# A streaming-encoder block on one core: operand offsets modulo 512 bytes, and four early steps of the output projection

## The chip, the cores and the metric

The kernel runs on one core of a Trainium2 chip. Its five engines have instruction streams of their own: TensorE (PE; its weight loads are listed apart as PEld), VectorE (DVE), ScalarE (ACT), GpSimd (POOL) and SyncE (SP), which here only issues transfers. The metric is the device time of one execution in microseconds, the median of the runs. All matmuls here have fp32 operands that were split into a high and a low fp32r part, so that each product is three matmuls: high·high, high·low, low·high.

## The reference

One Mamba-2 (SSD) mixer and one squared-ReLU MLP, each post-normalised, on a sequence of 1024 tokens with model width 1024:

```
h  = x * (1 + sc1) + sh1
zxbcdt = h @ w_in                      # 1024 -> 2048 (z) + 4096 (x, B, C) + 32 (dt)
xbc = silu(conv4(xbc)); dt = softplus(dt + bias)
y  = chunked SSD scan, 16 chunks of 64, 8 groups; y = y + d_skip * xs
y  = gated_rmsnorm(y, z) ; y = y @ w_out          # 2048 -> 1024
x  = layer_norm(ALPHA * x + g1 * y)
h  = x * (1 + sc2) + sh2
x  = layer_norm(ALPHA * x + g2 * (relu(h @ w1)**2 @ w2))   # 1024 -> 4096 -> 1024
```

The vectors sh, sc and g come from `silu(c) @ ada_w + ada_b`, which the kernel computes too, in blocks, beside the other work.

## The kernel before, in words

**Stages.** The head (to about 72 us) modulates x and computes dt. Then the input projection runs to about 725 us: 45 column tiles of `w_in` on line L146 (left operand `hi` or `lo`, right operand `hh` or `hl`, the split h), with the scan of group after group between its matmuls (L332 to L384) and a gate per half group (L392 to L420), which writes y to DRAM. The last gates, (7,0) and (7,1), run after the last projection; the gate's sum over channels is a pair of matmuls `pr` (L404, L405) on `sh` and `sl`.

**The output projection** follows, in four passes of `out_pass(T, Dh, po)`: T is the half of the tokens, Dh the half of the output columns. A pass has 16 steps k of 128 channels, each 12 matmuls of 128x512 on L559: four token tiles by three products, `lhsT` a piece of y, `rhs` the weights. Steps 14 and 15 come together at the end, since they need the last gates. `out_load` brings a step's weights (`owr`, 256 KB) and y (`yr`) in over SP; ScalarE casts the high part (L119), GpSimd subtracts for the low part of the weights (`owl`, L122), VectorE for that of y. y's split tiles are called `b11`, `b21` and so on after the blocks in which they lie: the same memory later holds h2, the MLP's input. In pass (0,0) the first two steps don't use `out_load`: their weights and y (both called early, `yx`) are loaded before the projection ends, into buffers of the projection's own pool.

Pass (0,1) does the other columns for the same tokens. It loads y's steps 0 and 1 again, now as `b` tiles. Beside it run two blocks of the modulation, `mods_ln1` (L594 to L607): 8 loads `adm`, a chain of 8 VectorE instructions (L600, L602), and then four one-column matmuls on L606 whose right operand is a column of ones. The tiles of `adm` share 8 buffers, so the second block's loads wait until the first block's chain and matmuls have read them. Passes (1,0) and (1,1) take the other tokens, with y in plain tiles `y0_k`, `y1_k` for k below 8 and in `b` tiles above.

**The MLP.** The first two weight tiles of `w1` are loaded and split into `w1h`, `w1l` by `forms1` (GpSimd subtracts, L122) while pass (1,1) runs. L713 then multiplies plainly, with some weights in tiles `ph`, `pl`; L804 has the larger part of the up-projection, in products of sums of blocks (7 products in place of 8, operands `t..`, `s..`, `b..`, `w1..`, 1176 matmuls); L918 has the down-projection, from about 1270 us.

**What sets the order.** Instructions are written in the order of the code, with a list `work` that is popped between projection tiles; the scheduler then orders each engine's stream by its own estimate, and a tile's buffer (pool, tag, `bufs`) makes its next user wait for its last reader. `issue_after(x)` keeps an instruction behind x.

**Where operands lie.** [...] The place of an operand in it modulo 512 bytes, of the left one against the right one, is as follows in the program built: L146 480/480, L918 both equal (480, 96 or 256), L559 with `b` tiles equal, L713 with `ph`, `pl` equal. Unequal are L804 (224 bytes apart, all 1176 matmuls), L713 with `w1h`, `w1l` (224 apart, 96 matmuls), L559 with the plain `y` tiles of passes (1,0) and (1,1) (224 apart, 192 matmuls), the early steps with `yx` (288 apart, 24 matmuls) and the head's L230 (288 apart, 160 matmuls). In most pairs of the first kind both operands lie in the same half of the partition's memory, in most of the second in different halves; L230's both lie in the upper half.

## Time and profile before

| | us |
|---|---|
| median of 3 runs (lowest, highest) | 1626.96 (1625.54, 1627.66) |
| the profiled execution | 1625.36 |
| its span | 1623.6 |
| TensorE busy | 1564.5 |
| VectorE, ScalarE, GpSimd busy | 984.7, 784.0, 561.4 |
| pass (0,0): first matmul to last | 725.6 to 787.9 |
| pass (0,1) | 787.9 to 839.6 |
| passes (1,0) and (1,1) | 839.6 to 931 |

The profile shows one execution, so durations are summed against its 1625.36 us, 1.6 us below the median. TensorE's matmuls are pipelined: the listed length of one (0.39 or 0.40 us) is longer than the distance from one start to the next, and it is the distance that counts in a row of them. Idle time of TensorE stands in the view of waits with what ended it. The granted clock is 1.00 at 2.4 GHz and 0.50 at 1.2 GHz.

### The profile page before, as it was taken

Reading aid. Unit: us, or ns where it says so; the run is one execution under the profiler, and the core shown is the slowest. Engines: PE = TensorE matmul, PEld = TensorE weight load, DVE = VectorE, ACT = ScalarE, POOL = GpSimd, SP = SyncE. Lnnn points to the kernel's source line nnn. Section 1 sums busy time; section 2 is a strip of 40 time slices with the busy share of each in tenths; the row PEclk is TensorE's granted clock in tenths of the full one; section 3 lists DMA queues with packets and bytes.
Section 4 is the critical chain, followed back from the end, with each engine's and each line's share of the span. In section 5 each row is a group of like instructions: output and inputs, shape, how many; then the busy total and the mean of one; then the engine's idle time right before and its main releaser. Section 6 shows DMA issues by size and latency. Waiting matters only on the chain.

```text
span 1623.6 us, 20290 instructions
## 1 busy us (share of the span) xinstructions
PE 1564.5 (96%) x7600; PEld 1263.0 (78%) x7600; DVE 984.7 (61%) x1473; ACT 784.0 (48%) x1183; POOL 561.4 (35%) x306
## 2 busy tenths in 40 slices
PE   6999999999999999998999999999999999999997
PEld 5887777878787888875787877888888888878886
DVE  8757886676768656747853356655554642296335
ACT  3546587575757676865334236333333323233230
POOL 3323424242333333244446607233332222244121
PEclk9999999999999999998999999999999999999999
DMA  8324422322323222215856413333334555436531
GB/s 323 138 76 135 143 98 79 104 88 83 116 66 121 67 88 64 79 33 169 287 165 210 130 65 104 118 115 105 104 117 159 205 183 175 151 139 224 172 124 52
DMA packets 78193, 209.89 MB, mean 129 GB/s; under 512 B 9744, under 2 KB 11280, under 8 KB 77200
## 3 DMA queue, kind: packets, MB, share of 16 engines
q1 hardware_dynamic: 76752, 204.91, 37.8%
q0 software_dynamic: 1056, 3.67, 0.6%
q8 instruction: 60, 0.98, 0.2%
q14 instruction: 37, 0.30, 0.1%
q10 hardware_dynamic: 288, 0.03, 0.0%
HBM read 175.41 MB, written 33.16 MB: 128 GB/s over the span
## 4 chain that ended last, share of the span: by engine, by line
PE 76%; DVE 10%; DMA 6%; ACT 4%; issue 2%; POOL 1%; SPq 0%; DVEq 0%; POOLq 0%; ACTq 0%
PE mm L146 22%; PE mm L918 20%; PE mm L804 17%; PE mm L559 6%; PE mm L713 3%; DMA adr<-in_ada_r_dram 2%; DVE mac L437 2%; PE py L364 2%; PE pst L377 1%; PE py L369 1%; PE mm L230 1%; DVE xs L159 1%; DMA yr<-y_dram 1%; DVE macc L205 1%; DMA ada<-in_ada_a_dram 1%
## 5 line engine op out<-in xcount | busy, mean ns | idle before, releaser
L146 PE MATMUL mm<-hh,whi 128*128 128x512 f32 x720 | 288.1, 400 | 0.0
L146 PE MATMUL mm<-hl,whi 128*128 128x512 f32 x720 | 286.4, 398 | 0.0
L146 PE MATMUL mm<-hh,wlo 128*128 128x512 f32 x720 | 286.1, 397 | 0.0
L918 PE MATMUL mm<-w2h,uh 128*128 128x512 f32 x512 | 197.9, 389 | 1.2 <-DVE tm L953 1.2
L918 PE MATMUL mm<-w2l,uh 128*128 128x512 f32 x512 | 198.2, 389 | 0.0
L918 PE MATMUL mm<-w2h,ul 128*128 128x512 f32 x512 | 197.1, 389 | 0.0
L122 POOL TENSOR_TENSOR wlo<-wraw,whi 128x1024 fp32r<-128x1024 f32 (+1 forms) x47 | 113.6, 2419 | 224.4 <-ACT whi L119 224.4
L146 PEld LDWEIGHTS mm<-hl,whi 128*128 128x128 f32 x720 | 136.4, 190 | 29.7 <-issue 2.2
L146 PEld LDWEIGHTS mm<-hh,whi 128*128 128x128 f32 x720 | 136.3, 189 | 29.3 <-issue 2.1
L146 PEld LDWEIGHTS mm<-hh,wlo 128*128 128x128 f32 x720 | 136.2, 189 | 28.8 <-issue 2.1
L358 POOL TENSOR_TENSOR ea<-ea,Ct 128x512 f32<-128x512 f32 x56 | 78.4, 1399 | 183.7 <-ACT ea L357 144.8
L122 POOL TENSOR_TENSOR w2l<-w2r,w2h 128x1024 fp32r<-128x1024 f32 x30 | 75.5, 2520 | 185.1 <-ACT w2h L119 185.1
L122 DVE TENSOR_TENSOR ul<-ur,uh 128x512 fp32r<-128x512 f32 x62 | 50.2, 818 | 125.8 <-ACT uh L119 125.6
L122 POOL TENSOR_TENSOR owl<-owr,owh 128x512 fp32r<-128x512 f32 x62 | 87.6, 1422 | 82.9 <-ACT owh L119 82.8
L918 PEld LDWEIGHTS mm<-w2h,uh 128*128 128x128 f32 x512 | 96.1, 188 | 21.7 <-DVE tm L953 1.6
L119 ACT CAST uh<-ur 128x512 fp32r<-128x512 f32 x62 | 38.3, 621 | 153.2 <-PE mm L918 124.3
L352 ACT ACTIVATE dec<-ar,acs 128x128 f32<-128x128 f32 x256 | 81.6, 390 | 62.5 <-PE py L364 59.2
L918 PEld LDWEIGHTS mm<-w2l,uh 128*128 128x128 f32 x512 | 96.1, 188 | 20.1
L918 PEld LDWEIGHTS mm<-w2h,ul 128*128 128x128 f32 x512 | 96.1, 188 | 19.7
L159 DVE SCALAR_TENSOR_TENSOR xs<-mm,convw,xs 128x1023 f32<-128x1023 f32 (+2 forms) x45 | 57.5, 1278 | 35.4 <-ACT xs L153 34.7
L119 ACT CAST owh<-owr 128x512 fp32r<-128x512 f32 x62 | 38.2, 619 | 78.3 <-PE mm L559 38.0
L119 ACT CAST w2h<-w2r 128x1024 fp32r<-128x1024 f32 x62 | 64.8, 1048 | 23.3 <-DMA w2r<-in_w_dram 18.2
(407 smaller groups left out, 3493.8 us busy)
## 6 DMA issues: line engine op xcount, KB each, us to landing
w2r<-in_w_dram SPq DMA_DIRECT2D x62, 512.0 KB, 3.8
wraw<-in_w_in_dram SPq DMA_DIRECT2D x45, 512.0 KB, 3.9
w1r<-in_w_dram SPq DMA_DIRECT2D x34, 512.0 KB, 3.7
ar<-a_dram SPq DMA_DIRECT2D x64, 256.0 KB, 3.2
owr<-in_w_out_dram SPq DMA_DIRECT2D x62, 256.0 KB, 3.1
ur<-u_dram SPq DMA_DIRECT2D x62, 256.0 KB, 2.8
u_dram<-row SPq DMA_DIRECT2D x28, 512.0 KB, 3.8
adr<-in_ada_r_dram SPq DMA_DIRECT2D x24, 512.0 KB, 3.5
```

Source lines behind the costliest of these rows:

```text
L119: return (act.copy if eng is act else eng.tensor_copy)(hi, src)
L122: return eng.tensor_tensor(lo, src, hi.bitcast(F32), op=ALU.subtract)
L146: pe.matmul(ps[:, hf, :], lhsT=w_[:, k, :], rhs=x_[:, k, ts], start=(k == 0 and i == 0), stop=(k == KT - 1 and i == 2))
L159: vec.scalar_tensor_tensor(dst[:, j:S], src[:, 0:S - j], convw[:, ct, 3 - j:4 - j], dst[:, j:S], op0=ALU.mult, op1=ALU.add)
L352: act.activation(dec[:, h, :], ar[:, h, :], AF.Relu, scale=-1.0, bias=acs[:, c, g * HPG + h:g * HPG + h + 1])
L358: pool.tensor_tensor(ea, ea, G["C"][:, ts].unsqueeze(1).broadcast_to([P, HPG, C]), op=ALU.mult)
L364: pe.matmul(py[i * HD:(i + 1) * HD, j, :], lhsT=X[:, h, :], rhs=dec[:, h, :], start=True, stop=(c == 0))
L437: vec.scalar_tensor_tensor(acc, ad[:, i, :], csil[:, k:k + 1], acc, op0=ALU.mult, op1=ALU.add)
L559: mm_ = pe.matmul(po[t // 2][:, t % 2, :], lhsT=l_[:, t * P:t * P + P], rhs=r_, start=(k == 0 and i == 0), stop=(k == 15 and i == 2))
L713: pe.matmul(ups[T, f // 2][:, f % 2, :], lhsT=w_[:, k, :], rhs=x_[:, k % 4, :], start=(k == 0 and i == 0), stop=(k == KT - 1 and i == 2))
L804: pe.matmul(dst, lhsT=w_[:, k, :], rhs=x_[:, k, :], start=(first and k == 0 and i == 0), stop=(k == 3 and i == 2), skip_group_check=not first)
L918: pe.matmul(po[t][:, Dh, :], lhsT=l_[:, t * P:(t + 1) * P], rhs=r_[:, Dh * 512:Dh * 512 + 512], start=(f == 0 and i == 0), stop=(f == NF - ...
```

## The change

1. **Offsets.** A function `offset(pool, n)` puts a tile of n bytes ahead in a pool (and clears it with one VectorE instruction): 288 bytes in the head's pool `hdp`, 224 in `mpa`. In the program built, L804, L713, L559 with `y` tiles and L230 then have their two operands at equal offsets modulo 512 bytes. The early steps' pairs stay 288 apart, and there are now 48 such matmuls.
2. **Four early steps.** Steps 0 to 3 of pass (0,0) are loaded and split ahead of the projection's end (tiles `wx`, `yx`); `wx` of step 0 and 1 share their buffers with the raw loads of steps 3 and 2, and `wx` of 2 and 3 take the tags of `whi` and `wlo`. Steps 4 to 7 of that pass are loaded into `spare` tiles, which have the memory of `b11`. `b11` is taken after the pass, so y's steps 0 to 3 (two more than before) are loaded and split again in pass (0,1).
3. **The table.** After the last projection's Silu, ScalarE loads the table that has both Ln and Exp.
4. **L606** (now L636) must come behind step 13 of its pass.
5. **`forms1`** lets VectorE make `w1l` of the first two tiles.

The listings below are one engine's instructions in program order: row number, line, operation, output and inputs. TensorE behind the projection, before: the end of the two steps on `yx` (24 matmuls from row 2861), then the pair `pr` of the next half gate, and step 2 on `b11`.

```order
2873 L559 MATMUL mm<-whi,yx 128x512
2874 L559 MATMUL mm<-wlo,yx 128x512
2875 L559 MATMUL mm<-whi,yx 128x512 x2
2876 L559 MATMUL mm<-wlo,yx 128x512
2877 L559 MATMUL mm<-whi,yx 128x512
2878 L404 MATMUL pr<-sh,ones_r 128x512
2879 L405 MATMUL pr<-sl,ones_r 128x512
2880 L559 MATMUL mm<-owh,b11h 128x512 x2
2881 L404 MATMUL pr<-sh,ones_r 128x512
2882 L559 MATMUL mm<-owl,b11h 128x512 x2
2883 L559 MATMUL mm<-owh,b11l 128x512
```

The same place now:

```order
2860 L410 MATMUL pr<-sl,ones_r 128x512
2861 L585 MATMUL mm<-wx,yx 128x512 x12
2862 L585 MATMUL mm<-wx,yx_6312 128x512 x6
2863 L585 MATMUL mm<-wx,yx_6313 128x512 x2
2864 L585 MATMUL mm<-wx,yx 128x512 x12
2865 L585 MATMUL mm<-wx,yx_6312 128x512 x6
2866 L585 MATMUL mm<-wx,yx_6313 128x512 x10
2867 L409 MATMUL pr<-sh,ones_r 128x512
2868 L585 MATMUL mm<-owh,b21h 128x512 x2
2869 L410 MATMUL pr<-sl,ones_r 128x512
2870 L585 MATMUL mm<-owl,b21h 128x512
```

Forty-eight matmuls in a row stand between the last gate pair of the projection and the next one, where 24 stood; the third `pr` pair, which stood two matmuls behind the second, stands at row 2899, 30 rows on.

TensorE in pass (0,1) before, where the first four one-column matmuls of the modulation stand (the second four are at row 3162):

```order
3110 L559 MATMUL mm_6797<-owh,b21h 128x512
3111 L559 MATMUL mm_6797<-owl,b21h 128x512
3112 L559 MATMUL mm_6797<-owh,b21l 128x512
3113 L606 MATMUL mm<-one_131,adm 128x1 x4
3114 L559 MATMUL mm_6796<-owh,b21h 128x512
3115 L559 MATMUL mm_6797<-owh,b21h 128x512
3116 L559 MATMUL mm_6796<-owl,b21h 128x512
```

The same four now, behind step 13 of the pass:

```order
3189 L585 MATMUL mm_6792<-owh,b22l 128x512
3190 L585 MATMUL mm_6791<-owh,b22h 128x512
3191 L585 MATMUL mm_6792<-owh,b22h 128x512
3192 L636 MATMUL mm<-one_131,adm 128x1 x4
3193 L585 MATMUL mm_6791<-owl,b22h 128x512
3194 L585 MATMUL mm_6791<-owh,b22l 128x512
```

They moved from the first third of the pass to its last steps. The second four now, where pass (1,0) begins on `y_0`:

```order
3213 L585 MATMUL mm_6792<-owl,b22h 128x512
3214 L585 MATMUL mm_6792<-owh,b22l 128x512
3215 L636 MATMUL mm<-one_131,adm 128x1 x4
3216 L585 MATMUL mm<-owh,y_0_7269 128x512
3217 L585 MATMUL mm<-owl,y_0_7269 128x512
```

They are the last instruction of pass (0,1), and the rows between the two fours hold 22 matmuls.

GpSimd in passes (1,0) and (1,1), before (`h_n` is a tile of h2, `owl` the low part of a step's weights):

```order
108 L122 TENSOR_TENSOR b21l<-h_7207,b21h 128x512
109 L122 TENSOR_TENSOR b21l<-h_7224,b21h 128x512
110 L122 TENSOR_TENSOR owl<-owr,owh 128x512 x3
111 L122 TENSOR_TENSOR w1l<-w1r,w1h 128x1024
112 L122 TENSOR_TENSOR owl<-owr,owh 128x512
113 L122 TENSOR_TENSOR w1l<-w1r,w1h 128x1024
114 L122 TENSOR_TENSOR b21l<-h_7241,b21h 128x512
115 L122 TENSOR_TENSOR b21l<-h_7258,b21h 128x512
116 L122 TENSOR_TENSOR owl<-owr,owh 128x512 x16
```

The same place of GpSimd now:

```order
108 L126 TENSOR_TENSOR b21l<-h_7210,b21h 128x512
109 L126 TENSOR_TENSOR b21l<-h_7227,b21h 128x512
110 L126 TENSOR_TENSOR owl<-owr,owh 128x512 x4
111 L126 TENSOR_TENSOR b21l<-h_7244,b21h 128x512
112 L126 TENSOR_TENSOR b21l<-h_7261,b21h 128x512
113 L126 TENSOR_TENSOR owl<-owr,owh 128x512 x16
```

It has nothing but `owl` and `b21l` left there. VectorE in the same passes now, where `forms1`'s two subtractions went:

```order
863 L126 TENSOR_TENSOR b11l<-h_7236,b11h 128x512
864 L123 CAST b11h<-h_7253 128x512
865 L126 TENSOR_TENSOR b11l<-h_7253,b11h 128x512
866 L126 TENSOR_TENSOR w1l<-w1r,w1h 128x1024
867 L577 TENSOR_TENSOR owr<-owr,g1b 128x512
868 L126 TENSOR_TENSOR w1l<-w1r,w1h 128x1024
869 L577 TENSOR_TENSOR owr<-owr,g1b 128x512 x2
870 L680 TENSOR_TENSOR tm<-mm,g1b 128x512 x2
```

They are its rows 866 and 868: VectorE makes `w1l` ahead of the multiplications `owr*g1b` of pass (1,1)'s weights.

The diff:

```diff
--- before.py
+++ after.py
@@ -47,6 +47,10 @@
 
     def const(shape, name, dt=F32):
         return con.tile(shape, dt, name=name, tag=name)
+
+    def offset(pl_, n):
+
+        vec.memset(pl_.tile([P, n // 4], F32, name="offset", tag="offset", bufs=1), 0.0)
 
     phA = ExitStack()
     ca = phA.enter_context(tc.tile_pool(name="ca", bufs=1, reuse_waits="tile"))
@@ -166,6 +170,7 @@
     hd = ExitStack()
     psh = hd.enter_context(tc.tile_pool(name="psh", bufs=1, space=PSUM))
     hdp = hd.enter_context(tc.tile_pool(name="hdp", bufs=2, reuse_waits="tile"))
+    offset(hdp, 288)
     hring = gp.tile([P, 2, S], F32, name="hring", tag="zt", bufs=1)
     hps = [psm.tile([P, 2, 512], F32, name="mm", tag="mm") for _ in range(2)]
     hps.append(psh.tile([P, 2, 512], F32, name="mmh", tag="mmh"))
@@ -453,7 +458,10 @@
         if j == 0:
             groups[g]["z"] = gp.tile([P, 2, S], F32, name="zt", tag="zt", bufs=1)
         ps = proj(2 * g + j)
-        act.activation(groups[g]["z"][:, j, :], ps.rearrange("p a b -> p (a b)"), AF.Silu)
+        sz = act.activation(groups[g]["z"][:, j, :], ps.rearrange("p a b -> p (a b)"), AF.Silu)
+        if (g, j) == (NG - 1, 1):
+            with tc.issue_after(sz.ins):
+                act.preload_act_table_set("natural_log_exp_and_others")
 
     work = []
 
@@ -488,16 +496,30 @@
         pop(int(debt))
         debt -= int(debt)
 
-    yx = gp.tile([P, 2, S], F32R, name="yx", tag="xs")
+    yx = [gp.tile([P, 2, S], F32R, name="yx", tag="xs"), gp.tile([P, S], F32R, name="yx2", tag="Bt"),
+          gp.tile([P, S], F32R, name="yx3", tag="Ct")]
+    raws = [None] * 4
+    wx = [None] * 4
+
+    def early_load(k):
+        raws[k] = wp.tile([P, 2, 512], F32, name="wraw", tag="wraw", bufs=4)
+        sp.dma_start(raws[k][:, 0, :], a["w_out"][k][:, 0:512])
+        sp.dma_start(raws[k][:, 1, :], y_dram[k][:, 0:512])
+
     early = []
-    for k in range(2):
-        raw = wp.tile([P, 2, 512], F32, name="wraw", tag="wraw", bufs=4)
-        sp.dma_start(raw[:, 0, :], a["w_out"][k][:, 0:512])
-        sp.dma_start(raw[:, 1, :], y_dram[k][:, 0:512])
-        w = [wp.tile([P, 512], F32R, name="w" + q, tag="w" + q) for q in ("hi", "lo")]
-        y = (yx[:, k, 0:512], yx[:, k, 512:S])
-        split(raw[:, 0, :], *w, act, pool)
-        split(raw[:, 1, :], *y, act, vec)
+    early_load(0)
+    early_load(1)
+    for k in range(4):
+        tg = "wraw" if k < 2 else "whi" if k == 2 else "wlo"
+        wx[k] = wp.tile([P, 2, 512], F32R, name="wx", tag=tg, **(dict(bufs=4) if k < 2 else {}))
+        if k == 1:
+            early_load(2)
+            early_load(3)
+    for k in range(4):
+        w = (wx[k][:, 0, :], wx[k][:, 1, :])
+        y = [(yx[0][:, k, :] if k < 2 else yx[k - 1])[:, i * 512:i * 512 + 512] for i in range(2)]
+        split(raws[k][:, 0, :], *w, act, pool)
+        split(raws[k][:, 1, :], *y, act, vec)
         early.append((w, y))
     phR.close()
 
@@ -510,7 +532,9 @@
 
         return [per.tile([P, 4, 512], F32R, name=nm + q, tag=nm + q) for q in "hl"]
 
-    B = {(kh, T): h2_block(f"b{kh + 1}{T + 1}") for T in range(2) for kh in range(2)}
+
+    spares = [per.tile([P, 4, 512], F32, name="spare" + q, tag="b11" + q) for q in "hl"]
+    B = {(kh, T): h2_block(f"b{kh + 1}{T + 1}") for T in range(2) for kh in range(2) if T + kh}
 
     def rstd_of(pl_, var, n, nm):
 
@@ -539,11 +563,13 @@
     def out_load(T, Dh, k):
 
         ds_ = slice(Dh * 512, Dh * 512 + 512)
-        wr = ob_pool.tile([P, 512], F32, name="owr", tag="owr", bufs=3)
+        spare = T == 0 and Dh == 0 and 4 <= k < 8
+        wr = (spares[0][:, k - 4, :] if spare else
+              ob_pool.tile([P, 512], F32, name="owr", tag="owr", bufs=3))
         queue["w"] = sp.dma_start(wr, a["w_out"][k][:, ds_]).ins
         yr = None
-        if (Dh == 0 and not (T == 0 and k >= 14)) or (T == 0 and k < 2):
-            yr = ob_pool.tile([P, 512], F32, name="yr", tag="yr")
+        if (Dh == 0 and not (T == 0 and k >= 14)) or (T == 0 and k < 4):
+            yr = spares[1][:, k - 4, :] if spare else ob_pool.tile([P, 512], F32, name="yr", tag="yr")
             sp.dma_start(yr, y_dram[k][:, T * 512:T * 512 + 512])
         wh = ob_pool.tile([P, 512], F32R, name="owh", tag="owh", bufs=3)
         wl = ob_pool.tile([P, 512], F32R, name="owl", tag="owl", bufs=3)
@@ -564,7 +590,7 @@
     def out_pass(T, Dh, po):
         ws = []
         for k in range(16):
-            first = T == 0 and Dh == 0 and k < 2
+            first = T == 0 and Dh == 0 and k < 4
             ws.append(early[k][0] if first else out_load(T, Dh, k))
             ks = [k] if k < 16 - KL else range(16 - KL, 16) if k == 15 else []
             for t in range(4):
@@ -573,10 +599,12 @@
             if Dh == 0 and T == 1 and k % 4 == 0:
                 load_row(4 + k // 4)
 
-    yt0 = yt = [y_tiles(0, k) for k in range(16)]
+    yt0 = yt = [None] * 4 + [y_tiles(0, k) for k in range(4, 16)]
     po = [psm.tile([P, 2, 512], F32, name="mm", tag="mm") for _ in range(2)]
     pop(len(work))
     out_pass(0, 0, po)
+    B[0, 0] = h2_block("b11")
+    yt[0:4] = [y_tiles(0, k) for k in range(4)]
     sbA.close()
     phA.close()
 
@@ -584,6 +612,7 @@
     lnp = ctx.enter_context(tc.tile_pool(name="lnp", bufs=1, reuse_waits="tile"))
     up_ = ExitStack()
     mpa = up_.enter_context(tc.tile_pool(name="mpa", bufs=2, reuse_waits="tile"))
+    offset(mpa, 224)
     rowp = up_.enter_context(tc.tile_pool(name="rowp", bufs=4, reuse_waits="tile"))
     hk = up_.enter_context(tc.tile_pool(name="hk", bufs=1, reuse_waits="tile"))
     q7t = lambda: hk.tile([P, 512], F32, name="q7", tag="q7")
@@ -602,8 +631,9 @@
                 vec.scalar_tensor_tensor(t_, t_, csil[:, k:k + 1], ad[-1], op0=ALU.mult, op1=ALU.add)
             ad.append(t_)
         pm = psm.tile([P, 2, 512], F32, name="mm", tag="mm")
-        for i in range(4):
-            pe.matmul(pm[:, 0, i:i + 1], lhsT=ad[-1][:, i * P:(i + 1) * P], rhs=one1, start=True, stop=True)
+        with tc.issue_after(queue["k13"]):
+            for i in range(4):
+                pe.matmul(pm[:, 0, i:i + 1], lhsT=ad[-1][:, i * P:(i + 1) * P], rhs=one1, start=True, stop=True)
         mod2_add(b, pm[:, 0, 0:4])
 
     rows = {}
@@ -685,7 +715,7 @@
     po = [psm.tile([P, 2, 512], F32, name="mm", tag="mm") for _ in range(2)]
     out_pass(1, 0, po)
     out_evict(1, 0, po, sts)
-    ws1 = [forms1(load1(f)) for f in range(2)]
+    ws1 = [forms1(load1(f), eng=vec) for f in range(2)]
     po = mm2()
     out_pass(1, 1, po)
     out_evict(1, 1, po, sts)
```

## Rows read from the trace of the kernel before

**Rows 1.** The page's first part: busy time, share of the span, instructions.

```profile
PE 1564.5 (96%) x7600; PEld 1263.0 (78%) x7600; DVE 984.7 (61%) x1473; ACT 784.0 (48%) x1183; POOL 561.4 (35%) x306
```

**Rows 2.** Windows of lines L804 and L918: length, PE busy (x), PEld busy (x), clock, DMA.

```profile
987.00:1270.00 283.00, 275.14 (x1176) 220.82 (x1176) 1.00 0.34 118
...
1290.00:1600.00 310.00, 308.80 (x1362) 255.35 (x1362) 1.00 0.48 161
```

**Rows 3.** Timeline of TensorE, lines L713 and L230: start us, us, instruction.

```profile
970.89 0.40 PE L713 MATMUL mm<-b12h,w1h 128*128 128x512 f32 x1
...
972.06 0.40 PE L713 MATMUL mm<-b12l,w1h 128*128 128x512 f32 x1
...
984.66 0.39 PE L713 MATMUL mm<-b12h,ph 128*128 128x512 f32 x1
...
986.02 0.39 PE L713 MATMUL mm<-b22h,ph 128*128 128x512 f32 x1
...
48.23 0.39 PE L230 MATMUL mm<-hh,wh 128*128 128x512 f32 x1
...
50.80 0.40 PE L230 MATMUL mmh<-hh,wl 128*128 128x512 f32 x1
```

**Rows 4.** Waits of TensorE from 700 to 1000 us: in total, times, longest.

```profile
PE mm L559 <- POOL owl L122: 3.7, 2, 3.1
PE mm L559 <- ACT b11h L119: 3.6, 1, 3.6
...
PE mm L606 <- DVE adm L602: 2.9, 1, 2.9
PE pr L404 <- DVE sh L119: 2.7, 2, 1.6
...
PE pr L405 <- DVE sl L122: 1.4, 1, 1.4
...
PE mm L559 <- POOL wlo L122: 0.6, 1, 0.6
```

**Rows 5.** Windows of line L559 in three stretches at half clock: columns as in Rows 2.

```profile
736.80:747.00 10.20, 5.33 (x11) 3.64 (x12) 0.50 0.29 91
...
808.50:811.90 3.40, 3.40 (x9) 2.66 (x8) 0.50 0.99 333
...
887.00:890.40 3.40, 2.95 (x7) 2.37 (x8) 0.50 0.37 93
```

**Rows 6.** Windows, all engines: PE, PEld, DVE, ACT, POOL busy, clock, DMA share, GB/s.

```profile
725.60:787.90 62.30, 53.70 (x248) 40.63 (x247) 42.22 (x58) 37.29 (x63) 31.42 (x25) 0.92 0.52 165
787.90:839.60 51.70, 47.80 (x209) 38.76 (x208) 34.00 (x42) 14.74 (x26) 22.82 (x16) 0.97 0.72 249
729.00:747.00 18.00, 9.52 (x25) 5.97 (x25) 13.26 (x18) 9.85 (x16) 7.41 (x8) 0.72 0.36 118
```

**Rows 7.** Timeline of ScalarE around the last projection: start, us, instruction, idle before.

```profile
724.88 1.03 ACT L456 ACTIVATE zt<-mm 128x1024 f32<-128x1024 f32 x1 [7.09 <-PE mm L146]
```

**Rows 8.** DMA issues between 780 and 850 us: KB each, median us to landing.

```profile
adm<-in_ada_r_dram SPq DMA_DIRECT2D x16, 256.0 KB, 5.2
```

**Rows 9.** Timeline of VectorE, the modulation chain, and its last rows before 890 us.

```profile
797.88 8.19 DVE L602 SCALAR_TENSOR_TENSOR adm<-adm,csil 128x512 f32<-128x512 f32 x7
...
886.30 1.64 DVE L551 TENSOR_TENSOR owr<-owr,g1b 128x512 f32<-128x512 f32 x1 [6.09 <-POOL b21l L122]
```

**Rows 10.** Timeline of GpSimd, 877 to 889 us.

```profile
877.26 2.40 POOL L122 TENSOR_TENSOR w1l<-w1r,w1h 128x1024 fp32r<-128x1024 f32 x1 [2.21 <-ACT w1h L119]
...
881.33 2.39 POOL L122 TENSOR_TENSOR w1l<-w1r,w1h 128x1024 fp32r<-128x1024 f32 x1
883.68 2.50 POOL L122 TENSOR_TENSOR b21l<-h,b21h 128x512 fp32r<-128x512 f32 x2
886.13 2.95 POOL L122 TENSOR_TENSOR owl<-owr,owh 128x512 fp32r<-128x512 f32 x2
```

**Rows 11.** Timeline of ScalarE, the cast that one of those subtractions waits for.

```profile
879.88 1.14 ACT L119 CAST b21h<-h 128x512 fp32r<-128x512 f32 x2
```

## The prediction

> **What bounds the kernel now.** I read the page's busy times first, and the reader is to see one number: TensorE works 1564.5 of 1623.6 us, 96% [rows 1]. So an edit pays only if TensorE's matmuls come closer together, if one of its idle gaps closes, or if a stretch at half clock goes. I then read three views for these three.
>
> For the distance I read windows of single lines. L804 is busy 275.14 us for 1176 matmuls, 234.0 ns each; L918, with the same shape and the same full clock, 308.80 us for 1362, 226.7 ns [rows 2]. TensorE doesn't wait in either, so something else parts them. The timeline has both values on one line: on L713 five distances with `w1h`, `w1l` take 972.06 − 970.89 = 1.17 us (234 ns), six with `ph`, `pl` 986.02 − 984.66 = 1.36 us (227 ns) [rows 3]. The left operands are of the same kind there; what differs is where the right one lies. L230 has eleven distances in 50.80 − 48.23 = 2.57 us, 234 ns, though both its operands lie in the same half [rows 3].
>
> For the gaps I read TensorE's waits from 700 to 1000 us. Those that the change touches are 8.3 us behind the projection (`b11h` 3.6, `sh` 2.7, `sl` 1.4, `wlo` 0.6), 2.9 for L606 on the `adm` chain, and one of 3.1 for `owl` [rows 4]. Around the first group 18.00 us hold only 9.52 of matmuls [rows 6]. With each of the three groups goes a stretch at clock 0.50, which is 1.2 GHz [rows 5].
>
> **The change part by part.**
>
> *Offsets.* Pairs at equal offsets go at 227 ns and pairs 224 or 288 bytes apart at 234, wherever I looked. I take 6.6 ns a matmul (1.40 against 1.36 us for six, between the rounded starts of [rows 3]); the busy times of [rows 2] would make it 7.3, but L804's hold its ramp after a wait. L804 gives 1176 × 6.6 ns = 7.8 us, L713's 96 matmuls with `w1` 0.6, the 192 with `y` tiles 1.3. The 24 early matmuls more that stay 288 apart cost 0.2. L230's 160 would give 1.1 us, of which I count nothing, because I have no row that makes that line the end of the head. The sum is 9.5. Its ends are 0, if the offset isn't the cause, and, at 7.3 ns for all 1440 (1176 + 96 + 192 − 24) and with L230's 160, 1600 × 7.3 ns = 11.7.
>
> *Four early steps.* The gaps of 8.3 us stand where TensorE has run out of early matmuls (24 × 0.23 = 5.6 us of them) while the last gates take ScalarE and VectorE in turns and steps 2 and 3 wait for casts behind these. With 48 it has 11.2 us of work from 725.6, to 736.8. All five waits of the group lay between 729 and 747 [rows 4, 6]. The second `pr` pair is now asked for at 736.8, in the middle of that, and the third 30 rows on, some 7 us later, so both find their operands there or nearly. The half clock of 736.8 to 747.0 covers 5.33 us of busy time [rows 5], half of which is lost: 2.7. What goes is 8.3 + 2.7 = 11.0.
> What is late next is step 4. Its two loads go into memory that the projection's last matmul reads, so SP stands there until about the Silu's start, 724.88 [rows 7], and the loads behind them too; then ScalarE's cast comes behind the gate's chain, and GpSimd's `owl` behind two issues of y's writes, which need VectorE. I put a gap of 2 us against this, and no half clock, since the gaps before were a cluster of five [rows 4]: 9.0 gained. The ends are 11.0 and 3.
> The extra splits (two more steps: four casts of 512 columns on ScalarE, two subtractions each on GpSimd and VectorE) come before the last projection's Silu, where ScalarE was idle for 7.09 us waiting for TensorE [rows 7]; that hides them. If a raw load is late there, ScalarE's queue stands in front of it, with the scan's exponentials behind. The table load moves 1.28 us of ScalarE's from the gate into the same idle time; nothing is counted. The two steps of y loaded again in pass (0,1) add 1 MB to about 12.9 MB (249 GB/s times 51.7 us) [rows 6] and two splits to a VectorE that is busy 34.0 of 51.7 us: nothing is counted, since both stay under the pass.
>
> *L606.* Behind step 13 its 2.9 us wait for the `adm` chain goes, since the chain has some 30 us more. The stretch of 3.40 us at half clock after it is busy throughout, and costs 1.7. What is late next is the second L606: 22 matmuls (22 × 0.227 = 5.0 us) behind the first, and its chain can't end until one `adm` load, which needs the buffer that the first reads, has landed (5.2 us [rows 8]) and one chain instruction has run (8.19 / 7 = 1.2 us with its waits [rows 9]). That is 6.4 against 5.0; I take a new gap of 1.0. The gain is 2.9 + 1.7 − 1.0 = 3.6, between 0 (a gap of 3 with a half clock behind it) and 4.6.
>
> *`w1l` on VectorE.* The 3.1 us wait is for `owl`, which GpSimd makes behind `w1l` (2.40 us), an `owl`, `w1l` again (2.39) and two `b21l` (2.50) [rows 10]. Without the two `w1l` the `b21l` wait for ScalarE's casts, which end at 879.88 + 1.14 = 881.02 [rows 11]; two of 1.25 and an `owl` of 1.27 bring the awaited one to about 884.8, where TensorE asked at 884.3: 0.5 remains. VectorE takes the two up in 6.09 us in which it was idle there [rows 9]. Half of the 2.95 us busy at half clock [rows 5] goes too, 1.5. The gain is 3.1 − 0.5 + 1.5 = 4.1, between 0 (VectorE stands for `w1r` in front of `owr*g1b`, and the wait changes its name) and 4.6.
>
> [...]
>
> **The sum.** 9.5 + 9.0 + 3.6 + 4.1 = 26.2 us. From the profiled execution's 1625.4 this leaves 1599.2; the median of the runs is 1.6 above it, which gives 1601.
>
> **The rivals.**
>
> 1. *The distance hangs on something else than the offset.* In the program built most equal pairs also lie in one half of the partition and most unequal ones in two, and that doesn't change. For it: this can't be parted on L713. Against it: L230, both in one half and 234 ns [rows 3]. Then 16.7 us are gained: 1610.
>
> 2. *The gaps come back behind the moved work.* Steps 4 and 5 come late by SP's stand, the gap after 736.8 is 5 to 6 us and TensorE falls to half clock again (3 gained in place of 9.0), and the second L606 waits 3 us and brings its half clock (0 in place of 3.6). For it: three gaps of 2.9 to 3.6 us have each a stretch at 0.50 with them [rows 4, 5]. Against it: 11.2 us of early work cover more than a load and two casts. The gain is 9.5 + 3 + 4.1 = 16.6: 1610 as well.
>
> 3. *Slower: pass (0,0) becomes bound by its loads.* Before, SP had step 2's loads out ahead of the projection's end; now everything behind step 4 waits for that end, so 12 steps of 0.52 MB come after 725. A step is 12 matmuls, 2.7 us, and needs 0.52 / 2.7 = 194 GB/s. The pass had 165 GB/s in the mean, and 118 in 729 to 747 [rows 6]. At 118 a step takes 4.4 us: 12 × 1.7 = 20 us lost and the 9.0 not gained, 1601 + 29 = 1630. It decides from about 120 GB/s down. For it: those two means. Against it: they are what the pass asked for, with the channel idle between; pass (0,1) got 249 [rows 6].
>
> 4. *No change:* rivals 1 and 2 together with `w1l`'s wait under a new name (0 of 4.1): 3 us gained, 1624, or within the 0.2% (3.3 us) that a measurement here can tell from nothing.
>
> **How the numbers follow.** My forecast has 0.68, rivals 1 and 2 have 0.12 each, rival 3 has 0.05 and 4 has 0.03. Faster by over 0.2%: 0.68 + 0.24 = 0.92; within: 0.03; slower: 0.05. The forecast's own range is from all upper ends (11.7 + 11.0 + 4.6 + 4.6 = 31.9: 1595) to one small part failing (1601 + 5 = 1606). The range of 8 in 10 goes on to rivals 1 and 2, at 1610, and leaves out 3 and 4: 1594 to 1612.
>
> **What would show it.** The offsets: L804 between 987 and 1270 (some 17 us earlier) at 227 ns a matmul, about 267 us in all; if it still reads 234, rival 1. The early steps: 48 matmuls with no wait from the projection's end on, one gap of about 2 us for `owl` or `sl`, and clock 1.00 there; a wait for a cast of step 4 and 0.50 after it is rival 2, waits for `owh` all along the pass with loads that land late rival 3. L606: no wait of L559 for it in the first third, and one of about 1 us on `adm` at the end. `w1l`: the wait for `owl` at 0.5 and no half clock before pass (1,1). If TensorE's waits in the scan before 725 grow by more than 2 us, the extra casts weren't hidden, and my cover for them is wrong.

## The result, and the profile after

The changed kernel takes 1609.34 us in the median of 4 runs (1606.65 to 1613.32), against 1626.25 before: a ratio of 0.9896 with a 95% interval of [0.9881, 0.9912]. It is faster, by 17 us where 25 were forecast. Its profiled execution took 1610.15 us, with a span of 1608.0.

The page's first part:

```profile
PE 1551.9 (97%) x7600; PEld 1261.4 (78%) x7600; DVE 988.9 (61%) x1479; ACT 784.1 (49%) x1184; POOL 555.9 (35%) x304
```

TensorE is busy 12.6 us less than in [rows 1] and idle 3 us less. Two windows of one line each answer to [rows 2] (stretch, length, PE busy with the count, PEld busy, clock, DMA share, GB/s):

```profile
979.20:1239.00 259.80, 258.54 (x1140) 213.58 (x1138) 1.00 0.34 117
...
1250.00:1590.00 340.00, 336.24 (x1483) 278.30 (x1483) 1.00 0.49 166
```

The products of sums, now L834, go at 258.54 us for 1140 matmuls, 226.8 ns each; L948 stays at 226.7. The same stretch of the kernel before, from the first of these matmuls to the first of the down-projection, which began at 1254.6 us, has as many:

```profile
987.40:1254.60 267.20, 266.24 (x1140) 213.86 (x1139) 1.00 0.33 114
```

That is 233.5 ns each. (The 234.0 read from [rows 2] has the last 36 too, which run singly between those of the down-projection.) The stretch takes 260.0 us (979.0 to 1239.0) where it took 267.2.

TensorE's waits from 720 to 1000 us, which answer to [rows 4]:

```profile
PE mm L585 <- POOL owl L126: 6.2, 5, 2.3
PE mm L636 <- DVE adm L631: 5.2, 1, 5.2
...
PE pr L410 <- DVE sl L126: 0.8, 1, 0.8
PE mm L585 <- ACT owh L123: 0.7, 2, 0.5
```

Of the 8.3 us behind the projection, 0.8 for `sl` is left, and one `owl` wait of 0.63 has come. L636, the old L606, waits for `adm` once and longer than it did: 5.2 us. The three passes in a row, which answer to [rows 6] (PE, PEld, DVE, ACT, POOL busy, clock, DMA share, GB/s):

```profile
723.70:778.48 54.78, 50.57 (x247) 39.17 (x246) 37.26 (x56) 33.24 (x57) 26.71 (x20) 1.00 0.54 173
778.48:832.15 53.67, 47.24 (x210) 38.26 (x208) 38.39 (x43) 16.49 (x28) 24.59 (x18) 0.97 0.76 255
832.15:885.10 52.95, 50.68 (x226) 41.51 (x227) 28.25 (x47) 24.05 (x40) 28.21 (x20) 0.93 0.59 199
```

Pass (0,0) fell from 62.3 to 54.8 us. Pass (0,1) rose from 51.7 to 53.7. Pass (1,0) stayed at 52.9 (it was 52.5, from 839.6 to 892.1, and pass (1,1) ended at 941.4), though its `y` matmuls are quicker. The timeline of TensorE has the early steps in its first row, and further on the first four matmuls of L636 and the second four (each of them is two instructions in the trace, so a row has x8):

```profile
723.72 11.36 PE L585 MATMUL mm<-wx,yx 128*128 128x512 f32 x48
734.92 0.40 PE L409 MATMUL pr<-sh,ones_r 128*128 128x512 f32 x1
735.16 0.63 PE L585 MATMUL mm<-owh,b21h 128*128 128x512 f32 x2
736.62 0.49 PE L410 MATMUL pr<-sl,ones_r 128*128 128x512 f32 x1 [0.83 <-DVE sl L126]
737.75 0.50 PE L585 MATMUL mm<-owl,b21h 128*128 128x512 f32 x1 [0.63 <-POOL owl L126]
...
819.12 0.95 PE L636 MATMUL mm<-one,adm 128*128 128x1 f32 x8
...
830.41 1.87 PE L636 MATMUL mm<-one,adm 128*128 128x1 f32 x8 [5.19 <-DVE adm L631]
```

Forty-eight matmuls run in 11.36 us without a gap, 233 ns from one to the next (their operands stay 288 bytes apart), and two small gaps of 0.83 and 0.63 us follow at full clock. The last 5.19 us before 830.41 are the new loss, and it takes the clock with it:

```profile
828.80:835.70 6.90, 5.29 (x17) 4.53 (x18) 6.70 (x11) 2.75 (x6) 3.22 (x2) 0.51 0.45 141
```

At 0.51 TensorE was busy 5.29 us of these 6.90, half of it lost: 2.6 us, most of it already in pass (1,0).

What the second four waited for stands on two queues. SP's issues in the timeline (start, length, instruction):

```profile
820.37 0.86 SPq L569 DMA_DIRECT2D owr<-in_w_out_dram  x2
822.22 0.33 SPq L573 DMA_DIRECT2D yr<-y_dram  x1
822.65 0.37 SPq L569 DMA_DIRECT2D owr<-in_w_out_dram  x1
823.97 0.33 SPq L573 DMA_DIRECT2D yr<-y_dram  x1
824.36 0.42 SPq L627 DMA_DIRECT2D adm<-in_ada_r_dram  x1
```

VectorE in the timeline just before the second four:

```profile
829.00 0.69 DVE L126 TENSOR_TENSOR b22l<-yr,b22h 128x512 fp32r<-128x512 f32 x1 [0.64 <-ACT b22h L123]
829.61 0.75 DVE L631 SCALAR_TENSOR_TENSOR adm<-adm,csil 128x512 f32<-128x512 f32 x1
```

The first four ended at 819.12 + 0.95 = 820.07 and gave the buffer back. The load `adm` went out only at 824.36, 4.3 us later: in front of it on SP stood two `owr`, and then two `yr` that waited for their own buffers, with an `owr` between them. It landed about 4.7 us after that, VectorE's last `b22l` stood in front for half a microsecond more, and the chain's last instruction ended at 830.36.

### The profile page after: what moved, and what is told of

It is laid out like the page before. It is cut to its first block, busy times and chain, and to the rows that moved or that the text cites. A ratio compares the mean times of both kernels' runs of the same rounds, so it can differ in the third digit from the quotient of the medians.

```text
span 1608.0 us, 20281 instructions
## 1 busy us (share of the span) xinstructions
PE 1551.9 (97%) x7600; PEld 1261.4 (78%) x7600; DVE 988.9 (61%) x1479; ACT 784.1 (49%) x1184; POOL 555.9 (35%) x304
## 4 chain that ended last, share of the span: by engine, by line
PE 72%; DVE 12%; DMA 7%; issue 4%; ACT 3%; POOL 2%; SPq 0%; DVEq 0%; POOLq 0%; ACTq 0%
PE mm L150 22%; PE mm L948 21%; PE mm L834 17%; PE mm L585 3%; PE mm L743 3%; DMA adr<-in_ada_r_dram 2%; DVE mac L442 2%; PE py L369 2%; PE pst L382 1%; DVE macc L210 1%; PE py L374 1%; POOL owl L126 1%; DVE xs L163 1%; DMA yr<-y_dram 1%; DMA owr<-in_w_out_dram 1%
## 5 line engine op out<-in xcount | busy, mean ns | idle before, releaser
L948 PE MATMUL mm<-w2h,uh 128*128 128x512 f32 x512 | 197.9, 389 | 1.2 <-DVE tm L983 1.2
L948 PE MATMUL mm<-w2l,uh 128*128 128x512 f32 x512 | 198.2, 389 | 0.0
L948 PE MATMUL mm<-w2h,ul 128*128 128x512 f32 x512 | 197.1, 389 | 0.0
L126 POOL TENSOR_TENSOR wlo<-wraw,whi 128x1024 fp32r<-128x1024 f32 x45 | 110.4, 2454 | 216.4 <-ACT whi L123 210.3
L948 PEld LDWEIGHTS mm<-w2h,uh 128*128 128x128 f32 x512 | 96.1, 188 | 21.4 <-DVE tm L983 1.6
L948 PEld LDWEIGHTS mm<-w2h,ul 128*128 128x128 f32 x512 | 96.1, 188 | 20.1
L948 PEld LDWEIGHTS mm<-w2l,uh 128*128 128x128 f32 x512 | 96.1, 188 | 20.0
L126 POOL TENSOR_TENSOR owl<-owr,owh 128x512 fp32r<-128x512 f32 x56 | 79.7, 1433 | 83.4 <-ACT owh L123 83.3
L359 DVE TENSOR_TENSOR dec<-dec,cbm 128x512 f32<-128x512 f32 x64 | 54.8, 855 | 27.5 <-ACT dec L358 27.2
```

Source lines behind the costliest of these rows:

```text
L126: return eng.tensor_tensor(lo, src, hi.bitcast(F32), op=ALU.subtract)
L359: vec.tensor_tensor(dec, dec, cbm.unsqueeze(1).broadcast_to([P, HPG, C]), op=ALU.mult)
L948: pe.matmul(po[t][:, Dh, :], lhsT=l_[:, t * P:(t + 1) * P], rhs=r_[:, Dh * 512:Dh * 512 + 512], start=(f == 0 and i == 0), stop=(f == NF - ...
```

## The experiments

All times are medians with the ratio to the kernel before, measured beside it. Runs of one kernel spread over 3 to 8 us, part of it in the projection: it ended anywhere from 722.9 to 727.0 us in the profiles. So a difference of 3 us between two versions isn't told by their times; waits and stretches of the traces are read beside them. A stretch varies too. With the offsets alone, which change no matmul of pass (0,1), that pass took 53.4 us against 51.7: the same wait of 2.9 us was followed by 6.8 us of half clock in place of 3.4.

| kernel | median us | ratio, 95% interval |
|---|---|---|
| the change | 1609.3 | 0.9896 [0.9881, 0.9912] |
| offsets alone | 1617.1 | 0.9944 [0.9929, 0.9959] |
| early steps and table alone | 1615.8 | 0.9935 [0.9918, 0.9953] |
| `w1l` on VectorE alone | 1623.8 | 0.9982 [0.9969, 0.9995] |
| rule on L606 alone | 1628.2 | 1.0012 [1.0000, 1.0023] |
| the change without that rule | 1605.0 | 0.9865 [0.9844, 0.9886] |
| + buffer for `adm` | 1609.7 | 0.9896 [0.9879, 0.9913] |
| + four `yr` buffers | 1607.4 | 0.9872 [0.9853, 0.9891] |
| + both | 1603.1 | 0.9866 [0.9846, 0.9886] |
| + both, without the rule | 1606.5 | 0.9881 [0.9865, 0.9898] |
| + both, `b21l` on VectorE | 1605.9 | 0.9878 [0.9859, 0.9897] |

**Offsets alone.** An operand's offset is its byte address within a partition of the on-chip memory, here modulo 512. On the kernel before:

```diff
+    offset(hdp, 288)
...
+    offset(mpa, 224)
```

> The kernel before with the two offset tiles alone. Theory (the distance between matmuls hangs on the offsets modulo 512 bytes): 1464 matmuls at 6.6 ns and some of the head's, 9.7 us and up to 1.1: 1626.3 - 10 = 1616, with 227 ns a matmul in the products of sums and on the plain y tiles. Rival (the half of the memory, or something else that the rest of the change brought): 1626, with 233 ns there.

Measured: 1617.1, 9.1 us less (6.7 to 11.6). A window of the products of sums, there on L810:

```profile
988.70:1248.50 259.80, 258.54 (x1140) 213.51 (x1139) 1.00 0.33 116
```

226.8 ns, with nothing changed but two tiles of 288 and 224 bytes, which move their operands by no more than that within a partition: the halves of the memory in which they lie stay the same, and the first rival falls. It is the distance of the two offsets that counts, and not the place of one operand alone, since L918 in the kernel before has equal pairs at 480, 96 and 256 and is as quick [rows 2].

**Other distances.** The changed kernel with other sizes of the two tiles (one run each):

```diff
-    offset(hdp, 288)          # first kernel: 32      second: 224
-    offset(mpa, 224)          # first kernel: 96      second: 192
```

> The changed kernel with 96 bytes in place of 224 in mpa and 32 in place of 288 in hdp: the products of sums (L834) and the plain y tiles then have their operands 128 bytes apart modulo 512, the head's L235 256 apart. Read from the trace: ns from one matmul's start to the next. Theory (anything but equal modulo 512 is slow): 233 in L834 and L235. Rival 1 (the period is 256 bytes): 233 in L834, 227 in L235. Rival 2 (the period is 128 or less): 227 in both. Time by the first: 1609.3 + 9.7 = about 1619, if all 1464 matmuls are slow.

> The changed kernel with 192 bytes in mpa and 224 in hdp: L834 and the plain y tiles have their operands 32 bytes apart, L235 64 apart. Theory (anything but equal is slow): 233 ns in both, about 1619. Rival 1 (the cost grows with the distance): between 227 and 229 in L834. Rival 2 (pairs within 64 bytes count as equal): 227 in both, 1609.

Measured: 1619.9 and 1622.9. A window of L834 in the first, 128 bytes apart:

```profile
986.00:1250.00 264.00, 262.65 (x1126) 210.99 (x1124) 1.00 0.34 117
```

The head in the same kernel's timeline, 256 apart, first and last of 12:

```profile
47.58 0.39 PE L235 MATMUL mm<-hh,wh 128*128 128x512 f32 x1
...
50.08 0.39 PE L235 MATMUL mmh<-hh,wl 128*128 128x512 f32 x1
```

The window of L834 in the second, 32 apart:

```profile
986.00:1250.00 264.00, 264.00 (x1132) 212.09 (x1133) 1.00 0.33 113
```

And the second's head in the timeline, 64 apart, first and last of 12:

```profile
48.19 0.39 PE L235 MATMUL mm<-hh,wh 128*128 128x512 f32 x1
...
50.71 0.39 PE L235 MATMUL mmh<-hh,wl 128*128 128x512 f32 x1
```

128 apart L834 takes 233.3 ns, and 32 apart 233.2: the quick distance is lost at the smallest step, and the rivals by which 128 would be equal, or 32 nearly so, fall. But 256 apart the head has 2.50 / 11 = 227 ns, as if equal. So the first rival of the first kernel holds in the head: what counts repeats at 256 bytes, not only at 512. L834 at 256 was not tried. And 64 apart the head has 2.52 / 11 = 229 ns, which neither the theory (233) nor a rival of the second kernel gives; no run explains it.

**The early steps alone.** The changed kernel without the other three parts:

```diff
-    offset(hdp, 288)
-    offset(mpa, 224)
-        with tc.issue_after(queue["k13"]):
-    ws1 = [forms1(load1(f), eng=vec) for f in range(2)]
+    ws1 = [forms1(load1(f)) for f in range(2)]
```

> The kernel before with the four early steps and the table load alone (no offset tiles, no rule on the one-column matmuls, w1l on GpSimd). Theory: pass (0,0) falls from 62.3 to about 55 us as in the changed kernel, and the rest stays: 1626.3 - 7.5 = 1619. Rival (the gaps come back behind the moved work, in pass (0,1) with its two more steps of y): 1623 or more.

Measured: 1615.8, 10.6 us less (7.6 to 13.4). Pass (0,0) took 54.1 us there, 8.2 less, and no other stretch of the trace shows the rest; this profiled execution was itself 6.8 us under the one before. The wait of L606 (there L634) in pass (0,1) stayed, and grew:

```profile
PE mm L634 <- DVE adm L629: 4.4, 1, 4.4
```

It was 2.9 [rows 4]. A pass that starts earlier doesn't have its loads earlier.

**`w1l` alone.** On the kernel before:

```diff
-    ws1 = [forms1(load1(f)) for f in range(2)]
+    ws1 = [forms1(load1(f), eng=vec) for f in range(2)]
```

> The kernel before with w1l of the first two tiles on VectorE alone. Theory (as predicted): the wait for owl goes from 3.1 us to 0.5 and its half clock with it, 1626.3 - 4.1 = 1622. Rival (VectorE or ScalarE stands for the w1r loads, and owl behind b21l is as late): the wait stays over 2 us and the time at 1625 to 1627.

Measured: 1623.8, 2.9 us less (0.8 to 5.0). The awaited matmul in TensorE's timeline:

```profile
884.84 0.50 PE L559 MATMUL mm<-owl,b12h 128*128 128x512 f32 x1 [1.06 <-POOL owl L122]
```

The wait is 1.1 in place of 3.1, and the half clock that followed is gone: nearer to the theory (4.1) than to the rival. Of the size 0.6 us of waiting is missing; the part on `w1l` in the last section has what it hangs on.

**The rule on L606 alone.** On the kernel before:

```diff
-        for i in range(4):
+        with tc.issue_after(queue["k13"]):
+          for i in range(4):
             pe.matmul(pm[:, 0, i:i + 1], ...
```

> The kernel before with the rule on the one-column matmuls alone. As predicted: the 2.9 us and 1.7 at half clock go, 1.0 comes at the end of pass (0,1): 1626.3 - 3.6 = 1623. Theory now (the second block's last load waits for the first four matmuls, behind other issues on SP): a wait of 4 to 6 us on adm at the end of the pass with a half clock behind it, 1626.3 - 4.6 + 8 = about 1630.

Measured: 1628.2, no gain (0 to 3.7 us slower). Neither number was right. The wait on `adm` at the end was small; what came was another in the first third. TensorE's waits:

```profile
PE mm L559 <- ACT owh L119: 2.1, 1, 2.1
...
PE mm L607 <- DVE adm L602: 0.4, 1, 0.4
```

And a window over the first half of pass (0,1) (the last two columns are the DMA share and GB/s):

```profile
788.00:812.00 24.00, 20.31 (x85) 15.59 (x85) 23.38 (x26) 4.55 (x8) 9.67 (x7) 0.98 0.88 324
```

The transfers fill 0.88 of these 24 us, and the weights come late: 2.1 us of waiting for `owh` where 2.9 for `adm` stood. So the old gap had covered a late load. Why that load is late stands on SP's queue and on ScalarE (its idle time in brackets):

```profile
798.06 7.15 SPq L598 DMA_DIRECT2D adm<-in_ada_r_dram  x6
805.30 1.30 SPq L543 DMA_DIRECT2D owr<-in_w_out_dram  x1
...
809.46 0.62 ACT L119 CAST owh<-owr 128x512 fp32r<-128x512 f32 x1 [7.67 <-DMA owr<-in_w_out_dram]
```

The `owr` went out behind six `adm` of the second block, which for some 6 of these 7.15 us waited for VectorE's chain to free their buffers. In the kernel before the same six stand there from 798.64 to 805.64, and the `owr` follows at 805.73. From 800 to 811 us the transfers filled only 0.71 of the time. So it is the order of the queue that makes this load late, more than the rate of the transfers.

**The change without the rule.**

```diff
-        with tc.issue_after(queue["k13"]):
+        if True:
```

> The changed kernel without the rule that the one-column matmuls stand behind step 13 of their pass. Theory (one buffer): the gap in the first third returns at its old size, 2.9 us and 1.7 for the half clock, and the one of 5.2 + 3.4 at the end goes: 1609.3 + 4.6 - 8.6 = about 1605. Rival (paced by loads): the pass takes as long as with the rule, 1609, or longer by the returned gap, 1614.

Measured: 1605.0, as the theory has it, and 22 us under the kernel before, which is about what the other three parts give alone (9.1 + 10.6 + 2.9 = 22.6, each with an interval of some 2 to 3 us on either side). The interval overlaps that of the change at its edge, so the times alone don't settle what the rule costs. In the traces passes (0,1) and (1,0) together take 100.8 us without it and 106.6 with it, though the wait for `adm` in the first third came back larger than the theory had it: 3.5 us and 6.8 us of half clock.

**A buffer for the last `adm` tile.**

```diff
-            t_ = hk.tile([P, 512], F32, name="adm", tag=f"h2{k % 2}{k // 2}")
+            t_ = hk.tile([P, 512], F32, name="adm", tag="q7" if (b, k) == (3, 7) else f"h2{k % 2}{k // 2}")
```

> The changed kernel with one edit: the last of the second modulation block's eight adm tiles gets a buffer of its own (tag q7, unused until the up-projection), so its load no longer waits for the first four one-column matmuls. Theory (one buffer): the 5.2 us wait of the second four on adm at the end of pass (0,1) and the 6.8 us at half clock behind it go, 5.2 + 3.4 = 8.6 us: 1609.3 - 8.6 = about 1601, wait under 0.5 us. Rival (pass (0,1) is paced by its loads and by VectorE, with two more steps of y in it): the wait changes its name to a load or a split of the same pass, and the time stays within 2 us of 1609.

Measured: 1609.7, nothing gained. The wait on `adm` was gone and pass (0,1) took 47.0 us, as the theory has it, but pass (1,0) took 56.0, with a wait of 3.2 for `owh`. The two passes as windows:

```profile
778.20:825.20 47.00, 46.00 (x209) 37.45 (x207) 32.84 (x38) 14.87 (x25) 24.46 (x18) 1.00 0.79 277
825.20:881.20 56.00, 50.63 (x226) 40.96 (x226) 28.21 (x48) 25.71 (x41) 27.65 (x20) 0.94 0.60 199
```

ScalarE's timeline at the start of the second (in brackets the idle time before, and what ended it):

```profile
824.27 0.62 ACT L123 CAST b22h<-yr 128x512 fp32r<-128x512 f32 x1 [2.36 <-DMA yr<-y_dram]
826.59 0.62 ACT L123 CAST b22h<-yr 128x512 fp32r<-128x512 f32 x1 [1.70 <-DMA yr<-y_dram]
828.84 0.62 ACT L123 CAST b22h<-yr 128x512 fp32r<-128x512 f32 x1 [1.63 <-DMA yr<-y_dram]
829.37 0.61 ACT L123 CAST owh<-owr 128x512 fp32r<-128x512 f32 x1
```

Three casts `b22h` of y for later steps stand ahead of the cast `owh` that the next step needs, and each waits for a load, as the brackets say; these loads share two `yr` buffers. The rival had the total right: the wait changed its name.

**Four `yr` buffers, with the `adm` buffer and without.**

```diff
-              ob_pool.tile([P, 512], F32, name="yr", tag="yr")
+              ob_pool.tile([P, 512], F32, name="yr", tag="yr", bufs=4)
```

> The changed kernel with the buffer of its own for the last adm tile and four buffers for yr in place of two. In the run with the adm buffer alone the wait on adm was gone, but pass (1,0) then waited 3.2 us for a cast of weights (owh) that stood on ScalarE behind three casts of y (b22h), each behind a load that waits for one of two yr buffers. Theory (the casts of y are paced by the two buffers and stand in front): with four the 3.2 and 0.7 us and the half clock behind them go, 1609.7 - 3.9 - 3.4 = about 1602. Rival (both passes together are paced by the loads, whatever stands in front): the gap appears elsewhere in passes (0,1) and (1,0), which together stay at 103 us, and the time at 1607 or more.

> The changed kernel with four buffers for yr and no buffer of its own for the last adm tile. Theory (that tile's load waits for the first four matmuls, and for the issues that stand in front of it on SP, which wait for yr buffers): the wait on adm falls from 5.2 us to between 1 and 3, since only the second part goes, a half clock stays, and the time lies between 1603 (both edits) and 1609: about 1606. Rival (the adm buffer alone makes the wait): 5 us on adm as before, 1608 or more. Second rival (SP's queue alone): no wait on adm, 1603.

Measured: 1603.1 with both, as the theory has it, and 1607.4 with the `yr` buffers alone. The two passes with both, as windows:

```profile
779.28:827.85 48.57, 46.83 (x210) 37.35 (x208) 36.03 (x44) 17.36 (x31) 23.90 (x18) 1.00 0.83 288
827.85:876.47 48.62, 47.79 (x226) 39.28 (x226) 29.34 (x45) 23.31 (x38) 29.16 (x20) 1.00 0.55 194
```

Each takes 48.6 us at full clock. TensorE's wait on `adm` with the `yr` buffers alone:

```profile
PE mm L636 <- DVE adm L631: 0.5, 1, 0.5
```

It fell from 5.2 to 0.5 us without a buffer for the tile, and no half clock follows: SP's queue made nearly all of it, as the second rival had it. The time lies between, and the intervals of the two overlap; in the trace pass (1,0) took 52.8 us against 48.6, with three waits for `owl` and one for `owh` (4.3 us).

Five traces have the rule and the shared buffer of `adm`. In each the load can go when the first four matmuls have ended:

| kernel | first four end | load goes out | after | TensorE waits |
|---|---|---|---|---|
| the change | 820.07 | 824.36 | 4.29 | 5.2 |
| the change, operands 32 apart | 824.83 | 827.45 | 2.62 | 3.4 |
| the change, operands 128 apart | 824.53 | 824.82 | 0.29 | 1.2 |
| + four `yr` buffers | 823.78 | 823.84 | 0.06 | 0.5 |
| rule on L606 alone | 834.53 | 834.59 | 0.06 | 0.4 |

The third of them in SP's timeline, and its wait:

```profile
824.82 0.43 SPq L627 DMA_DIRECT2D adm<-in_ada_r_dram  x1
...
PE mm L636 <- DVE adm L631: 1.2, 1, 1.2
```

The wait goes with the time that the load stands on SP. TensorE has the same order of instructions in the first three, so the 5.2 us are the largest of three executions and not a fixed price; with SP free the wait is 0.4 to 1.2 us.

**Both buffers without the rule.** The two edits above, and:

```diff
-        with tc.issue_after(queue["k13"]):
+        if True:
```

> The version with both buffer edits (1603.1 us) without the rule that the one-column matmuls stand behind step 13. Theory (the rule is worth its predicted gain once its second wait is cured): the gap of 3.5 us on adm in the first third and up to 3.4 us of half clock return: 1603 + 4 to 7 = 1607 to 1610. Rival (that stretch of pass (0,1) is paced by its loads at some 400 GB/s, as the rule alone on the kernel before showed, where a 2.1 us wait for owh took the place of the 2.9 on adm): the time stays at 1602 to 1605, with waits for owh in the one and for adm in the other.

Measured: 1606.5. Pass (0,1) takes 48.51 us in it (779.33 to 827.84), 48.57 with the rule. TensorE's waits on `adm`:

```profile
PE mm L636 <- DVE adm L631: 2.0, 2, 1.4
```

They cost 2.0 us; with the rule 0.7 for `owh` and 0.8 for `owl` stand in that stretch, and the pass is as long: the rule gives nothing there, as the rival has it. The time lies between the rival's range (to 1605) and the theory's (from 1607), and the two versions' intervals overlap. The two profiled executions are 2.1 us apart, and pass (1,0) has it: 50.9 us without the rule, 48.6 with it. Whether the rule makes that is not shown.

**`b21l` on VectorE.** Both buffers, and:

```diff
-                queue["h2l"] = low(..., vec if kh == 0 or T == 1 else pool).ins
+                queue["h2l"] = low(..., vec).ins
```

> The same with the four low parts of h2 that GpSimd makes (b21l) moved to VectorE as well. In the changed kernel the awaited owl of pass (1,1) stood on GpSimd behind two b21l (3.28 us). Theory: that wait of 2.3 us (1.5 in the run with the adm buffer alone) goes, and its half clock where there is one: 1602 - 1.5 to 5 = 1597 to 1600. Rival (ScalarE's casts, behind the w1r loads, set that owl): under 0.5 us against the run without this edit.

Measured: 1605.9, no gain against 1603.1. At the end of pass (1,0) TensorE waits for no `owl` in either version; inside pass (1,1) one came 0.8 us late with this edit and 0.6 without it. So the wait that the theory meant to take had gone with the buffers, and the rival's reason wasn't put to the test.

## Why the prediction was right, and where it failed

The direction and the range held (1609.3 in 1594 to 1612). The forecast of 1601 was 8 us too low, and the measured time lies outside the forecast's own range (1595 to 1606): it is in the wider one because that goes on to rivals 1 and 2 at 1610. Of rival 2 one half came true, the second L606 with its wait and its half clock; the other half, a gap and a half clock behind the early steps, did not. Between the two profiled spans lie 15.5 us: 7.5 in pass (0,0), 7.3 in the products of sums, 1.4 in L713 and pass (1,1), less 2.4 in passes (0,1) and (1,0), and 1.9 of an earlier end of the projection, which no part of the sum had and which lies within its spread. So the terms that failed are larger than the 8 us show.

*Offsets:* 9.5 forecast, 9.1 measured alone. The distance per matmul came out as read from [rows 3]: 226.8, some 6.6 ns less than in the same stretch before, as was taken. The step was right, and more general than said (256 bytes, in the head). What I left out for the head was right to leave out as far as the traces tell: the projection began at 63.7 to 65.2 us in the eight with equal offsets there, and at 64.3 to 64.9 in the four without. The Trainium skill, "TensorE: Matmul & The Clock Gate", section "Back-to-back issue gap", gives a stream of weight loads and matmuls one spacing for a length, about 131 ns at 512 columns. Here the spacing is 226.8 and 233.5 ns at that length, by the offset, and the measurement decides.

*Four early steps:* 9.0 forecast, 7.5 in pass (0,0), 10.6 alone. The gap before step 4 was 0.83 + 0.63 = 1.5, where I took 2, at full clock. Not foreseen were 2.7 us at 763 to 770, where `owh` (0.5) and `owl` (1.2 and 1.0) come late for the last steps. The sign that I named against the hidden casts didn't come: TensorE's waits between 64 and 722 us came to 15.3 us, 16.2 before, and ScalarE was still idle for 5.0 us ahead of the last Silu, where it had been for 7.1.

*`w1l`:* 4.1 forecast, 2.9 alone, and 0.9 of waiting in the changed kernel (2.27 against 3.13). There the `owl` stands behind two `b21l` again, in GpSimd's timeline; the last row is VectorE's:

```profile
875.76 3.28 POOL L126 TENSOR_TENSOR b21l<-h,b21h 128x512 fp32r<-128x512 f32 x2 [0.18 <-ACT b21h L123]
879.00 2.98 POOL L126 TENSOR_TENSOR owl<-owr,owh 128x512 fp32r<-128x512 f32 x2
...
875.20 1.47 DVE L126 TENSOR_TENSOR w1l<-w1r,w1h 128x1024 fp32r<-128x1024 f32 x1 [0.98 <-ACT w1h L123]
```

The two `b21l` took 3.28 us in place of 2.50 [rows 10]. VectorE was busy with `w1l` at 875.20 to 876.67, and the traces go by that overlap. In five of them (this one, those with other distances, `w1l` alone, and the `adm` buffer) the first `b21l` starts while VectorE makes `w1l`: it takes 2.06 us in each, and that `w1l` 1.47. With the `yr` buffers alone, and with both buffers without the rule, `w1l` ended before, and the two `b21l` take 1.27 to 1.29 each and `w1l` 1.23. The two in the first of these, where `w1l` ended at 874.90:

```profile
876.00 2.52 POOL L126 TENSOR_TENSOR b21l<-h,b21h 128x512 fp32r<-128x512 f32 x2
```

So the move to VectorE slowed what it was to make room for, by some 0.8 us; the sum had two of 1.25. And the half clock behind the wait stayed in the changed kernel, in a window of all engines (columns as above):

```profile
880.00:883.45 3.45, 3.13 (x7) 2.48 (x8) 1.05 (x2) 0.00 (x0) 1.99 (x2) 0.51 0.39 110
```

*L606:* this step failed. I wrote "That is 6.4 against 5.0; I take a new gap of 1.0". The gap was 5.2, since the load, once its buffer was free, had SP's queue in front of it for 4.3 us; I had priced its landing (5.2 forecast, 4.7 found) and the chain, and not the queue that it stands in. Where SP was free the gap was 0.4 to 1.2, so the terms that I had priced hold. And the gain on the other side, 2.9 + 1.7, wasn't there to be had: the rule alone gives nothing, because the weights of that stretch stand on SP behind six `adm` and come late whichever instruction waits for them. So 3.6 forecast became a loss: 2.0 us in pass (0,1) and 1.75 of half clock in pass (1,0) until 835.65. These two sizes are those of one execution. Without the rule the kernel's median is 1605, and with `yr` buffers for SP's queue and the `adm` buffer 1603, which is near the forecast. "Nothing is counted" for y's two steps loaded again may be part of the same error, since these loads stand on the same queue; no run has them alone. With the early steps alone pass (0,1) took 52.2 us against 51.7, and its wait for `adm` grew from 2.9 to 4.4.

Rival 2 had this gap's size (3 us and its half clock) but not its cause, and its other half, a late step 4, didn't come. Rivals 1, 3 and 4 fell.

## What to carry to other kernels

Read the distance between the starts of matmuls of one shape, line by line: two values at one clock can mean operand addresses, and a pad of some hundred bytes cures it. When a wait is moved to a later place, list every issue that its load then stands behind on the loading engine; a queue that waits for other buffers costs more than the load. Before counting a gap as gain, ask what arrives during it: where transfers fill the stretch, another instruction waits in its place.

## What the runs showed of the hardware

At 2.4 GHz a 128x512 fp32r matmul starts 227 ns after the last when both operands lie at equal offsets modulo 512 bytes in their partitions, or 256 apart, and 229 to 234 ns after it at the other distances tried (32, 64, 128, 224, 288). At 128 apart the distance isn't steady: single ones of 229 to 230 and of 237 to 238 make up the mean of 233. What a gap costs beside its length changed from run to run: part of the half clock fell into the gap itself, as at 828.8, where TensorE stood until 830.4.
